# A decoder block on one Trainium2 core: v split in freed constants' space with the output steps overlapped, and two pairs of the embedding gate's second half by seven products

## The chip, the cores and the metric

The kernel runs on one core of one Trainium2 chip. A core has a matrix engine (PE, with its weight loads shown apart as PEld), a vector engine (DVE), a scalar engine (ACT), GpSimd (POOL) and SyncE (SP), which here only issues DMAs. SBUF is the on-chip memory the engines work from, PSUM the eight banks that matmuls accumulate in. The metric is the device time of one execution in microseconds (us); lower is better.

## The reference, cut to what matters

One decoder layer on x of 256 tokens by 2048 columns, all in float32. Two parts matter here. The first is the end of branch A, the gated linear attention, with 4 heads whose values are 512 wide:

```
o = gla_chunked(q, k, v, log_a)
o = o * lax.rsqrt(jnp.mean(o * o, -1, keepdims=True) + RMS_EPS) * gla_norm_g.astype(f32)
o = (o.reshape(B, S, GLA_V) * jax.nn.silu(gr.astype(f32))).astype(x.dtype)
y_gla = o @ w_branch_gla
```

The second is the very end of the layer, the per-layer embedding:

```
x = x + jax.nn.sigmoid(x @ w_ple_gate[i]) * (p[i] @ w_ple_proj[i])
```

Between them lie the second branch, the merge, the output projection, two layer norms and a gated MLP of width 5632. Ahead of the embedding stands the second layer norm, so that its x is the normalised result of the MLP.

## The kernel before, in words

**How a product is made.** Every float32 factor is split into a high part (ACT copies it to the matmul's reduced float32, `copy`, L112) and a low part (DVE subtracts, for weights in `prep`, L220). A product is then three matmuls: high by high, high by low, low by high. Weights come in 284 units of 128 rows by 2048 columns (1 MB). `prep` loads a unit as two halves of 512 KB over SP's queue into `raw` (5 buffers) and splits them into `hi` and `lo` tiles (6 buffers each). `unit(ahead=3)` hands out the next unit and prepares up to three ahead; a preparation starts when a `hi` tile comes free, that is when PE has finished with an older unit. SP works in the order written; the other engines' order is made by a planner, which takes the instruction that is ready by its own estimate of time, earlier program text first.

**Two ways to multiply.** Where weights are the moving operand, a unit is a pair of 128-row blocks by 1024 columns against two token blocks. The classic way (`x_mm`, L333, or `classic` in `s_half`, L792) is 2 x 2 x 2 block products of three matmuls, 24 matmuls of 512 columns. The other way (`strassen` in `s_half`) has seven block products instead of eight, 21 matmuls. It needs sums of activation blocks (`s_sums`, four DVE additions), differences of weight blocks (`differences`, L148, four DVE subtractions of 512 columns), and splits 3584 columns of weights instead of 2048 (`prep_s`, L194). Its products accumulate partly in four more PSUM banks `p1`, `p5`, `p6`, `p7`, which `fold` (L819) adds into an SBUF tile after the last such pair of a half; what the classic pairs gave is added by the evacuation. The projections `gv` and `gr`, the output projection `wo` and the MLP's `dn` are made so; the embedding's gate `pg` is not.

**The output steps of branch A.** After `gv` and `gr`, which fill `vg[h]` (v and the swish gate of head h), come the last 12 merge gates `psm` (n = 20 to 31). Each is 16 pairs of a 512-column and a 256-column matmul. Between their matmuls the generator `o_gen` is pulled one step at a time, twice per gate from n = 21. For each head in turn its steps are: `split` (v and the attention matrix into high and low parts: tiles `vs`, `ath`, `atl`), a pause, `product` (9 matmuls `go`; ACT squares and sums, DVE and POOL make the root, DVE scales and gates, L965), a pause, `turn` (8 PE transposes `gt`, then a split into `oT[h]`). One head is done before the next begins, 5 pulls each. `vs` is a tile of the pool `big`, 15 slots of 8 KB per partition that also hold xT (4 slots), `ofT` (2), the attention matrices (1), the gates `sg` (4), `vg` (4) and `oT` (4). A slot of `xT` is free when the last merge gate has read it. The branch projections `psa` follow and read `oT`.

**Constants' space.** Masks and other constants of the early stages lie in a pool `ec` that stays open until the merge gates are done; the norm's gain `gnb` is one of them.

**The embedding gate.** `pg` is two halves of 1024 columns, each 8 units, by `x_half`. The first half begins inside the second layer norm (`begin2`) and ends with the evacuation of its four banks: ACT's tanh from PSUM (L1460), two DVE steps (L1461, L1463), and a 256 KB store. The store is not issued there but kept in a list; `store_first` issues the four on SP's queue after the second half's first unit. In the second half the last two units are taken bank by bank, so that three banks are evacuated while PE works on the next. The fourth bank is split in two tiles of 256 columns (`fine`) for all eight units, so that its first half can be evacuated while PE makes the second. The last evacuation and its store end the program.

Of the kernel before, what the change touches and what calls it, by code (L numbers as in the profile page):

```python
# [9 lines left out]
F32 = mybir.dt.float32  # L10
# [9 lines left out]
P = 128  # L20
# [41 lines left out]
DN_T = ((3, 6, 9, 12, 15, 18), (5, 9, 12, 15))  # L62
AFF1 = ((0, 2, 3), (0, 2))
# [9 lines left out]
def tile_block(ctx: ExitStack, tc: tile.TileContext, wu, wfv, wpp, xT_in, x_in, pT_in, wlr,  # L73
# [17 lines left out]
    ec = early.enter_context(tc.tile_pool(name="ec", bufs=1))  # L91
    pmm = ctx.enter_context(tc.tile_pool(name="pmm", bufs=6, space=PSUM))
# [28 lines left out]
    for _ in range(8):  # L121
# [7 lines left out]
               for b, order, sset in ((52, WO_ORDER, GV_S), (68, WO_ORDER, GR_S),  # L129
                                      (120, OUT_ORDER, WO_S), (dn0, DN_ORDER, DN_S))  # L130
# [125 lines left out]
    gnb = ec.tile([P, 512], F32, name="gnb")  # L256
# [513 lines left out]
    def s_half(nm, nh, order, sset, cl, st, zof, ev, tail=0, mid={}, end=None, ahead=3,  # L770
               residual=True):
# [19 lines left out]
        def mm(ps, x, w):  # L791
            nc.tensor.matmul(ps, lhsT=x, rhs=w, start=todo[id(ps)] == total[id(ps)],  # L792
                             stop=todo[id(ps)] == 1)
            todo[id(ps)] -= 1
# [48 lines left out]

        if tail:
            end(tail_mm)
            return
# [59 lines left out]

    vg = [s8([P, 2, 2, 512], name=f"vg{h}") for h in range(H)]
# [28 lines left out]
    def o_gen():  # L936
        parts, ogs = {}, {}

        def split(h):
            vs = s8([P, 2, 2, 512], F32R, name=f"vs{h}")  # L940
            copy(vs[:, 0], vg[h][:, 0])
            nc.vector.tensor_tensor(vs[:, 1], vg[h][:, 0], vs[:, 0].bitcast(F32), ALU.subtract)
# [5 lines left out]
        def product(h):  # L948
            vs, ah, al = parts.pop(h)
            for t in range(2):  # L950
                po = mxtile(f"go{h}_{t}")
                ks = ((0, 0),) if t == 0 else ((256, 0), (128, 1))
                mm = [(x[:, o:o + P], vs[:, i, s, :]) for o, s in ks
# [23 lines left out]
        for h in range(H):  # L977
            split(h)
            yield
            yield  # L980
            product(h)
            yield
            yield
            turn(h)
            yield
# [12 lines left out]
    for n in range(PSM1, 32):  # L998
        merge_gate(n, lambda i: pull(1) if i in (3, 11) and n > PSM1 else None)
# [447 lines left out]
    stores = []  # L1447

    def store_first():
        for store in stores:  # L1450
            store()

    for nh in range(2):
        def ev_o(t, c, ps, ab=(0, 512), nh=nh):
            th = t2("tho")
            r = t2("res")
            e = slice(*ab)
            w = slice(c * 512 + ab[0], c * 512 + ab[1])
            o = slice(nh * 1024 + w.start, nh * 1024 + w.stop)
            nc.scalar.activation(th[:, e], ps, AF.Tanh, bias=0.0, scale=0.5)  # L1460
            nc.vector.scalar_tensor_tensor(th[:, e], th[:, e], 1.0, pp[nh][:, t, w],  # L1461
# [114 lines left out]
```

## Time and profile before

| | us |
|---|---|
| median of 3 runs | 1661.32 (1660.44 to 1662.15) |
| the profiled execution: its own time | 1661.22 |
| its span, first to last instruction | 1659.4 |
| PE busy | 1652.1 |
| PEld busy | 1434.6 |
| DVE busy | 1307.9 |
| ACT busy | 899.8 |
| POOL busy | 71.2 |

The span leaves out 1.8 us of the execution's time. Matmuls are pipelined and the profile models their ends, so a busy PE says little by itself: two matmuls that follow without a gap are shown overlapping, and a short wait can hide inside the overlap. What counts for PE is the distance between the starts of its matmuls. Names like `psm` or `go` are the program's tiles, with buffer numbers left out; `L965` is line 965 of the kernel.

### The profile page before, as it was taken

How to read it: one execution, taken by the hardware profiler on the slowest of the kernel's cores; microseconds unless marked ns; L12 is line 12 of the kernel's file. 1: busy time of each engine (PE TensorE's matmuls, PEld its weight loads, DVE VectorE, ACT ScalarE, POOL GpSimd, SP SyncE). 2: the span in 40 equal slices, each digit the busy share in tenths (PEclk: the TensorE clock that was granted, in tenths of full speed). 3: DMA queues.
4: the chain of work that ended last, by engine and by line, in shares of the span. 5: the costliest groups of instructions: out<-in, count | busy, mean ns of one | idle time of the engine just before them, and what ended most of it. 6: DMA issues, size and time to landing. Idle time of an engine off the chain costs nothing.

```text
span 1659.4 us, 24382 instructions
## 1 busy us (share of the span) xinstructions
PE 1652.1 (100%) x8917; PEld 1434.6 (86%) x8917; DVE 1307.9 (79%) x1983; ACT 899.8 (54%) x1314; POOL 71.2 (4%) x210
## 2 busy tenths in 40 slices
PE   9999999999999999999999999999999999999998
PEld 9988888888888888888898888888888888888887
DVE  7666877888889767888987877777777778988774
ACT  6655555555555654455575455555545556556543
POOL 0100000000000000000010101100111000000000
PEclk9999999999999999999999999999999999999999
DMA  8755555546566556878856877778677679898554
GB/s 322 254 165 169 170 175 173 185 158 201 199 205 203 186 187 250 307 241 306 314 172 204 274 269 268 265 243 290 241 263 253 237 268 339 288 363 312 177 187 156
DMA packets 103432, 391.61 MB, mean 236 GB/s; under 512 B 11736, under 2 KB 13024, under 8 KB 96400
## 3 DMA queue, kind: packets, MB, share of 16 engines
q1 hardware_dynamic: 98448, 363.83, 64.3%
q0 software_dynamic: 4864, 26.23, 4.2%
q8 instruction: 70, 1.15, 0.3%
q14 instruction: 50, 0.41, 0.1%
HBM read 362.74 MB, written 27.27 MB: 235 GB/s over the span
## 4 chain that ended last, share of the span: by engine, by line
PE 98%; DVE 1%; ACT 0%; issue 0%; POOL 0%; POOLq 0%; DVEq 0%; ACTq 0%
PE dn L792 10%; PE psu L287 10%; PE psg L287 9%; PE psm L287 7%; PE pg L333 5%; PE psu L289 5%; PE psg L289 5%; PE gv L792 4%; PE gr L792 4%; PE wo L792 4%; PE psm L289 4%; PE dn_p L792 3%; PE psa L287 3%; PE fv L452 3%; PE psfk L287 2%; PE psk L287 2%
## 5 line engine op out<-in xcount | busy, mean ns | idle before, releaser
L220 DVE TENSOR_TENSOR lo<-raw,hi 128x1024 fp32r<-128x1024 f32 x490 | 595.0, 1220 | 192.8 <-ACT hi L112 190.7
L112 ACT ACTIVATE hi<-raw 128x1024 fp32r<-128x1024 f32 x490 | 516.0, 1057 | 380.3 <-issue 143.5
L287 PE MATMUL psu<-x1T,hi 128*128 128x512 f32 x688 | 240.4, 392 | 0.0
L287 PE MATMUL psg<-x1T,hi 128*128 128x512 f32 x672 | 234.8, 392 | 0.0
L289 PE MATMUL psu<-x1T,lo 128*128 128x256 f32 x688 | 192.3, 280 | 0.0
L289 PE MATMUL psg<-x1T,lo 128*128 128x256 f32 x672 | 187.8, 280 | 0.0
L287 PE MATMUL psm<-xT,hi 128*128 128x512 f32 x512 | 181.4, 396 | 0.0
L287 PEld LDWEIGHTS psu<-x1T,hi 128*128 128x128 f32 x688 | 129.2, 188 | 27.6
L287 PEld LDWEIGHTS psg<-x1T,hi 128*128 128x128 f32 x672 | 126.2, 188 | 27.0
L289 PE MATMUL psm<-xT,lo 128*128 128x256 f32 x512 | 143.3, 280 | 0.0
L289 PEld LDWEIGHTS psu<-x1T,lo 128*128 128x128 f32 x688 | 130.6, 190 | 0.0
L289 PEld LDWEIGHTS psg<-x1T,lo 128*128 128x128 f32 x672 | 127.6, 190 | 0.0
L287 PEld LDWEIGHTS psm<-xT,hi 128*128 128x128 f32 x512 | 96.2, 188 | 19.7
L792 PE MATMUL dn<-hi,hC 128*128 128x512 f32 x368 | 102.3, 389 | 0.0
L289 PEld LDWEIGHTS psm<-xT,lo 128*128 128x128 f32 x512 | 97.1, 190 | 0.2
L112 ACT ACTIVATE hi_b<-raw 128x512 fp32r<-128x512 f32 x78 | 65.3, 841 | 53.5 <-DMA raw<-in_wu_dram 19.8
L112 ACT ACTIVATE hi_t<-raw 128x1024 fp32r<-128x1024 f32 x48 | 51.0, 1063 | 75.5 <-DVE raw L148 51.1
L287 PE MATMUL psa<-oT,hi 128*128 128x512 f32 x256 | 89.8, 392 | 0.0
L194 DVE TENSOR_TENSOR lo_b<-raw,hi_b 128x512 fp32r<-128x512 f32 x78 | 73.7, 952 | 15.4 <-ACT hi_b L112 15.3
L792 PEld LDWEIGHTS dn<-hi,hC 128*128 128x128 f32 x368 | 69.0, 188 | 14.4
L289 PE MATMUL psa<-oT,lo 128*128 128x256 f32 x256 | 71.6, 280 | 0.0
L333 PE MATMUL pg<-hi,x2T 128*128 128x512 f32 (+1 forms) x256 | 69.7, 380 | 0.0
(366 smaller groups left out, 3199.5 us busy)
## 6 DMA issues: line engine op xcount, KB each, us to landing
raw<-in_wu_dram SPq DMA_DIRECT2D x553, 512.0 KB, 5.1
td<-in_wu_dram SPq DMA_DIRECT2D x15, 1024.0 KB, 8.5
td<-td POOLq DMA_DIRECT2D x15, 1024.0 KB, 6.5
td<-td SPq DMA_DIRECT2D x15, 1024.0 KB, 8.2
hS<-sd SPq DMA_DIRECT2D x21, 512.0 KB, 8.2
fvraw<-in_wfv_dram SPq DMA_DIRECT2D x13, 524.0 KB, 6.6
sd<-hs POOLq DMA_DIRECT2D x24, 256.0 KB, 5.7
lnb<-in_lng_dram SPq DMA_DIRECT2D x4, 1024.0 KB, 10.3
```

The source lines that it names most:

```text
L112: return nc.scalar.activation(o, i, AF.Copy, bias=0.0, scale=scale)
L194: nc.vector.tensor_tensor(lo, src, hi.bitcast(F32), ALU.subtract)
L220: i = nc.vector.tensor_tensor(lo, raw, hi.bitcast(F32), ALU.subtract)
L287: nc.tensor.matmul(ps, lhsT=hi[i // 8 if hoff == 0 else 0][:, w0 % 1024:w0 % 1024 + P], rhs=a[:, kt % 4, :], start=first and i == 0, stop= ...
L289: nc.tensor.matmul(ps[:, 256:512], lhsT=lo[i // 8 if hoff == 0 else 0][:, w0 % 1024:w0 % 1024 + P], rhs=a[:, kt % 4, 0:256], start=False, ...
L333: nc.tensor.matmul(bs[j][:, 0:m], lhsT=x, rhs=v[:, o:o + m], start=first and i == 0, stop=last and i == 2)
L452: nc.tensor.matmul(fbk[t][c][:, 0:n], lhsT=x, rhs=w[:, o:o + n], start=kt == 0 and i == 0, stop=kt == 15 and i == 2)
L792: nc.tensor.matmul(ps, lhsT=x, rhs=w, start=todo[id(ps)] == total[id(ps)], stop=todo[id(ps)] == 1)
```

## The change

Three parts of the program are changed.

1. **Output steps.** The pool `ec` is cut in two: `gnb` stays, the other constants move to an inner pool that is closed before `gv`. In the freed space `split` now makes v's high part (`vh`, one buffer for both token blocks) and the low part of the first token block (`vl`); the low part of the second takes one of the six small tiles `t2`. No slot of `big` is used, and the subtraction is two of 512 columns instead of one of 1024. `o_gen` runs 19 steps in which heads overlap: head h is split at step 4h, multiplied at 4h + 2, turned at 4h + 5, with `turn` ahead of the other two within a step.
2. **Embedding gate's second half.** It goes through `s_half`, with pairs 2 and 4 by seven products. `g_sums` makes the sums of those pairs after unit 4 of the first half. The result is gathered in an SBUF tile `zg` (by `fold`), to which the evacuation `ev_g` adds each bank before the tanh. The fourth bank is one tile until the last two units; those put their upper 256 columns in a further bank `half`, which is added at the very end.
3. **First half's stores.** They are issued by GpSimd, each right after its evacuation, instead of four on SP's queue in the second half.

The weights are laid out on the host to match. The core of the diff:

```diff
 DN_T = ((3, 6, 9, 12, 15, 18), (5, 9, 12, 15))
+PG_ORDER = (tuple(range(8)), tuple(range(8)))
+PG_S = ((), (2, 4))
 AFF1 = ((0, 2, 3), (0, 2))
...
     ec = early.enter_context(tc.tile_pool(name="ec", bufs=1))
+    gnb = ec.tile([P, 512], F32, name="gnb")
+    first_ = ctx.enter_context(ExitStack())
+    ec = first_.enter_context(tc.tile_pool(name="ec2", bufs=1))
     pmm = ctx.enter_context(tc.tile_pool(name="pmm", bufs=6, space=PSUM))
...
                for b, order, sset in ((52, WO_ORDER, GV_S), (68, WO_ORDER, GR_S),
-                                      (120, OUT_ORDER, WO_S), (dn0, DN_ORDER, DN_S))
+                                      (120, OUT_ORDER, WO_S), (dn0, DN_ORDER, DN_S),
+                                      (NU - 16, PG_ORDER, PG_S))
                for nh in range(2) for i, n in enumerate(order[nh]) if n in sset[nh]}
...
     cmask = ec.tile([P, 256], F32, name="cmask")
-    gnb = ec.tile([P, 512], F32, name="gnb")
     reset = ec.tile([P, 256], F32, name="reset")
...
     def s_half(nm, nh, order, sset, cl, st, zof, ev, tail=0, mid={}, end=None, ahead=3,
-               residual=True):
+               residual=True, fine=False):
...
-        def mm(ps, x, w):
-            nc.tensor.matmul(ps, lhsT=x, rhs=w, start=todo[id(ps)] == total[id(ps)],
+        def mm(ps, x, w, e=slice(0, 512)):
+            nc.tensor.matmul(ps[:, e], lhsT=x, rhs=w, start=todo[id(ps)] == total[id(ps)],
                              stop=todo[id(ps)] == 1)
...
+        if fine:
+            for t, c in ((0, 0), (0, 1), (1, 0)):
+                for i in range(tail):
+                    tail_mm(t, c, i)
+            half = mmtile(f"{nm}{nh}_11b")[:, 0:256]
+            last = [(x, v[:, 512:1024]) for i in range(tail) for j in range(2)
+                    for ah, al in (cl(order[n - tail + i], j, 1),)
+                    for x, v in ((ah, us[i][0][j]), (ah, us[i][1][j]), (al, us[i][0][j]))]
+            for x, v in last:
+                mm(C[1][1], x, v[:, 0:256], slice(0, 256))
+            for k, (x, v) in enumerate(last):
+                nc.tensor.matmul(half, lhsT=x, rhs=v[:, 256:512], start=k == 0,
+                                 stop=k == len(last) - 1)
+            ev(1, 1, C[1][1], half)
+            return
         if tail:
...
+    first_.close()
+    ec = early.enter_context(tc.tile_pool(name="ec3", bufs=1))
     vg = [s8([P, 2, 2, 512], name=f"vg{h}") for h in range(H)]
...
         def split(h):
-            vs = s8([P, 2, 2, 512], F32R, name=f"vs{h}")
-            copy(vs[:, 0], vg[h][:, 0])
-            nc.vector.tensor_tensor(vs[:, 1], vg[h][:, 0], vs[:, 0].bitcast(F32), ALU.subtract)
+            vh = ec.tile([P, 2, 512], F32R, tag="vh", name=f"vh{h}")
+            copy(vh, vg[h][:, 0])
+            vl = [ec.tile([P, 512], F32R, tag="vl", name=f"vl{h}"),
+                  sm.tile([P, 512], F32R, tag="t2", bufs=6, name="vl1")]
+            for t in range(2):
+                nc.vector.tensor_tensor(vl[t], vg[h][:, 0, t], vh[:, t].bitcast(F32),
+                                        ALU.subtract)
+            vs = [(vh[:, t], vl[t]) for t in range(2)]
             ah, al = [sm.tile([P, 384], F32R, tag="t2", bufs=6, name=n) for n in ("ath", "atl")]
...
                 ks = ((0, 0),) if t == 0 else ((256, 0), (128, 1))
-                mm = [(x[:, o:o + P], vs[:, i, s, :]) for o, s in ks
+                mm = [(x[:, o:o + P], vs[s][i]) for o, s in ks
                       for x, i in ((ah, 0), (ah, 1), (al, 0))]
...
-        for h in range(H):
-            split(h)
-            yield
-            yield
-            product(h)
-            yield
-            yield
-            turn(h)
+        for k in range(19):
+            for f, o in ((turn, 5), (product, 2), (split, 0)):
+                h, r = divmod(k - o, 4)
+                if r == 0 and 0 <= h < H:
+                    f(h)
             yield
...
     for n in range(PSM1, 32):
-        merge_gate(n, lambda i: pull(1) if i in (3, 11) and n > PSM1 else None)
+        merge_gate(n, lambda i: pull(1) if i in (3, 11) and 2 * n + i // 8 > 2 * PSM1 + 1 else None)
     while mixers:
...
-    stores = []
-    def store_first():
-        for store in stores:
-            store()
-    for nh in range(2):
-        def ev_o(t, c, ps, ab=(0, 512), nh=nh):
-            th = t2("tho")
-            r = t2("res")
-            e = slice(*ab)
-            w = slice(c * 512 + ab[0], c * 512 + ab[1])
-            o = slice(nh * 1024 + w.start, nh * 1024 + w.stop)
-            nc.scalar.activation(th[:, e], ps, AF.Tanh, bias=0.0, scale=0.5)
-            nc.vector.scalar_tensor_tensor(th[:, e], th[:, e], 1.0, pp[nh][:, t, w],
-                                           ALU.add, ALU.mult)
-            nc.vector.scalar_tensor_tensor(r[:, e], th[:, e], 0.5, z2[nh][:, t, w],
-                                           ALU.mult, ALU.add)
-            store = lambda: nc.sync.dma_start(out[t, :, o], r[:, e])
-            if nh == 0:
-                stores.append(store)
-            else:
-                store()
-        x_half(f"pg{nh}", x2T, 16, ev_o, pulls=2, begin=begin2 if nh == 0 else None,
-               tail=2 if nh == 1 else 0, mid=((mid3, 4), (store_first, 0))[nh],
-               fine=nh == 1)
+    def put(z, nh, t, c, ab=(0, 512)):
+        th = t2("tho")
+        r = t2("res")
+        e = slice(*ab)
+        w = slice(c * 512 + ab[0], c * 512 + ab[1])
+        o = slice(nh * 1024 + w.start, nh * 1024 + w.stop)
+        nc.scalar.activation(th[:, e], z, AF.Tanh, bias=0.0, scale=0.5)
+        nc.vector.scalar_tensor_tensor(th[:, e], th[:, e], 1.0, pp[nh][:, t, w],
+                                       ALU.add, ALU.mult)
+        nc.vector.scalar_tensor_tensor(r[:, e], th[:, e], 0.5, z2[nh][:, t, w],
+                                       ALU.mult, ALU.add)
+        (nc.gpsimd if nh == 0 else nc.sync).dma_start(out[t, :, o], r[:, e])
+    def g_cl(pair, j, t):
+        kt = 2 * pair + j
+        a = x2T[kt // 4][:, kt % 4, :]
+        return a[:, t * P:t * P + P], a[:, 256 + t * P:256 + t * P + P]
+    gS_ = {}
+    def g_sums():
+        for i, pair in enumerate(PG_S[1]):
+            o = s8([P, 4, 256], F32R, name=f"gS{pair}")
+            a = x2T[pair // 2][:, pair % 2 * 2:pair % 2 * 2 + 2, :].bitcast(F32)
+            y = t2("gy").rearrange("p (k t) -> p k t", t=S)
+            nc.vector.tensor_tensor(y, a[:, :, 0:256], a[:, :, 256:512], ALU.add)
+            v = s_sums(y)
+            copy(o[:, :, 0:P], v)
+            nc.vector.tensor_tensor(o[:, :, P:256], v, o[:, :, 0:P].bitcast(F32), ALU.subtract)
+            gS_[pair] = o
+    def g_st(pair, i):
+        if i < 3:
+            return g_cl(pair, (0, 1, 1)[i], (0, 0, 1)[i])
+        return cell(gS_[pair], i - 3)
+    zg = s8([P, 2, 2, 512], name="zg")
+    def ev_g(t, c, ps, half=None):
+        z = zg[:, t, c, :]
+        es = (slice(0, 512),) if half is None else (slice(0, 256), slice(256, 512))
+        for e in es:
+            nc.vector.tensor_tensor(z[:, e], z[:, e], ps[:, e], ALU.add)
+        for e in es:
+            if e.start:
+                nc.vector.tensor_tensor(z[:, e], z[:, e], half, ALU.add)
+            put(z[:, e], 1, t, c, (e.start, e.stop))
+    def mid4():
+        mid3()
+        g_sums()
+    x_half("pg0", x2T, 16, lambda t, c, ps: put(ps, 0, t, c), pulls=2,
+           begin=begin2, mid=(mid4, 4))
+    s_half("pg", 1, PG_ORDER[1], PG_S[1], g_cl, g_st, lambda t, g: zg[:, t, g - 2, :], ev_g,
+           2, {}, residual=False, fine=True)
     assert n_used[0] == NU, (n_used[0], NU)
...
            _sst(i["w_down"][0], DN_ORDER, DN_S),
-           _xst(i["w_ple_gate"][0])], 0)
+           _sst(i["w_ple_gate"][0], PG_ORDER, PG_S)], 0)
     wfv = np.concatenate([c("fv", 1024), c("glr", 16), c("ff", 8)], 1)
```

## Prediction

> **What bounds the kernel now.** I read the page's engine totals first, then the chain that ended last.
>
> ```profile
> span 1659.4 us, 24382 instructions
> PE 1652.1 (100%) x8917; PEld 1434.6 (86%) x8917; DVE 1307.9 (79%) x1983; ACT 899.8 (54%) x1314; POOL 71.2 (4%) x210
> ...
> PE 98%; DVE 1%; ACT 0%; issue 0%; POOL 0%; POOLq 0%; DVEq 0%; ACTq 0%
> ```
>
> The chain is PE for 98% of the span, so a change pays in two ways only: by taking matmuls away, or by closing one of the few places where PE waits; and it costs where PE newly waits, or behind the last matmul. Next come the prices of a matmul, from the chain in order of time (start, length, what).
>
> ```profile
> 421.86 6.12 PE gv L792 x27
> ...
> 1641.28 1.71 PE pg L333 x8
> 1644.06 8.24 PE pg L333 x36
> ```
>
> 27 matmuls of 512 columns take 6.12 us, 0.227 us each, and three of the last four banks (36 matmuls) take 8.24, 0.229 each: PE runs without gaps in both. The row at 1641.28 is one 128-row block of the second gate half: from its start to 1644.06 are 2.78 us, where 12 x 0.227 = 2.72. The difference is the fourth bank, made as 2 x 256 columns.
>
> The Trainium skill, in "TensorE: Matmul & The Clock Gate", section "Wait — 56ns, not 53.3ns?", gives a matmul a fixed cost of about 2.5 ns beside its columns. By that page merging 36 pairs of 256 columns would be worth an estimated 36 x 2.5 ns = 0.09 us instead of the 0.72 worked out below, and my time would be 1659.7. The row shows 60 ns per 3 pairs, 20 ns each, so I go by the row.
>
> Then PE's own timeline around the output steps (the bracket is idle time and who ended it):
>
> ```profile
> 549.12 0.63 PE L956 MATMUL go<-vs,ath 128*128 128x512 f32 x2
> 550.18 0.50 PE L956 MATMUL go<-vs,atl 128*128 128x512 f32 x1 [0.43 <-DVE atl L945]
> ...
> 610.68 0.40 PE L287 MATMUL psm<-xT,hi 128*128 128x512 f32 x1
> 611.51 0.66 PE L974 MATMUL gt<-ident,og 128*128 128x128 f32 x4 [0.43 <-DVE gst L961]
> ...
> 612.36 0.28 PE L289 MATMUL psm<-xT,lo 128*128 128x256 f32 x1
> 613.05 0.66 PE L974 MATMUL gt<-ident,og 128*128 128x128 f32 x4 [0.41 <-DVE og L965]
> ...
> 619.70 0.39 PE L287 MATMUL psa<-oT,hi 128*128 128x512 f32 x1
> 620.39 0.66 PE L974 MATMUL gt<-ident,og 128*128 128x128 f32 x4 [0.30 <-DVE og L965]
> ```
>
> By starts, the last three waits cost 0.83 - 0.23 = 0.60, 0.69 - 0.11 = 0.58 and 0.69 - 0.23 = 0.46 us: 1.64 in all. The first, at head 0's product, costs 1.06 - 0.45 = 0.61. DVE and ACT show why the three stand together.
>
> ```profile
> 560.46 1.23 DVE L942 TENSOR_TENSOR vs<-vg,vs 128x1024 fp32r<-128x1024 f32 x1 [0.45 <-ACT vs L112]
> ...
> 605.88 1.06 ACT L112 ACTIVATE vs<-vg 128x1024 fp32r<-128x1024 f32 x1
> 607.00 1.21 DVE L942 TENSOR_TENSOR vs<-vg,vs 128x1024 fp32r<-128x1024 f32 x1
> ...
> 613.98 1.22 DVE L942 TENSOR_TENSOR vs<-vg,vs 128x1024 fp32r<-128x1024 f32 x1
> ```
>
> Head 1's `vs` is made at 560, head 2's not before 606, although v had been there since `gv` and a head takes five pulls, 8 matmul pairs apart (8 x 0.34 = 2.8 us). At that time the 15 slots of `big` hold xT 4, ofT 2, attention 1, sg 4, vg 2, oT 2: all 15. Head 2 gets a slot when the last merge gate has left the first part of xT, and heads 2 and 3 are squeezed into the end, each PE step right behind its DVE and POOL chain.
>
> **The change part by part. Output steps.** Without `vs` in `big` nothing waits for xT: head 2's product frees a `vg` slot, which `oT[2]` takes. At one pull per 2.8 us head 3's turn, step 17, comes near 600 us, inside the merge gates. Three steps, 8.3 us, now lie between product and turn. The chain between them, below, is 2.1 us from PE's start to `og`'s end for a whole bank (609.10 to 611.45 in the squeezed case, for the first token block), so the three waits, 1.64 us, should go. Against that: head h + 1's product now follows head h's turn after one step instead of three, and needs the two PSUM tiles that the turn used.
>
> ```profile
> 609.10 0.60 ACT L959 ACTIVATE sq<-go 128x512 f32<-128x512 f32 x1 [0.62 <-PE go L956]
> ...
> 610.70 0.75 DVE L965 SCALAR_TENSOR_TENSOR og<-go,gst,vg 128x512 f32<-128x512 f32 x1 [0.73 <-POOL gst L963]
> ...
> 557.45 1.04 PE L974 MATMUL gt<-ident,og 128*128 128x128 f32 x8
> 558.72 1.29 DVE L992 TENSOR_TENSOR oT<-gt,oT 128x512 fp32r<-128x512 f32 x2
> ```
>
> After a turn at 557.45 its tiles are read by 560.01, 2.6 us later; the next product would come 0.9 + 2.8 = 3.7 us after it. 1.1 us of slack covers one DVE split in front (1.23) almost, so I take 0 for this new wait and keep 3 x 0.5 us as its upper bound. Head 0's wait (0.61) is DVE being busy; the two subtractions of 512 that replace one of 1024 cost 2 x 0.69 against 1.23, and I leave that wait as it is, between 0 and 1.2. The part gives -1.6, between -2.3 and +0.5.
>
> **Embedding gate, PE.** Two pairs by 21 matmuls instead of 24 save 6 x 0.227 = 1.36 us. The fourth bank in one piece saves 0.06 x 12 blocks = 0.72; its last two units stay split. Together -2.1.
>
> **Embedding gate, the engines that feed PE.** A seven-product unit costs DVE three splits of 1024 and one of 512 and four differences, 3 x 1.23 + 0.69 + 4 x 0.69 = 7.1 us, against 2.5 classic: +9.3 for two. The sums cost 2 x (0.69 + 4 x 0.28 + 0.69) = 5.0, the fold 4 x 0.68 = 2.7; ACT gets under 5. The cover (window, its length, busy time of PE, PEld, DVE), and the rows of the small steps (mean ns behind the comma):
>
> ```profile
> 454.00:537.00 83.00, 83.00 (x369) 68.71 (x368) 75.65 (x89) 46.74 (x51) 0.00 (x0) 1.00 0.61 200
> ...
> 1588.00:1600.00 12.00, 12.00 (x56) 9.97 (x55) 11.33 (x15) 6.29 (x9) 0.00 (x0) 1.00 0.58 190
> 1600.00:1611.00 11.00, 11.00 (x51) 9.09 (x50) 5.79 (x6) 4.96 (x6) 0.00 (x0) 1.00 0.18 62
> 1611.00:1622.00 11.00, 11.00 (x60) 9.34 (x59) 5.51 (x8) 2.76 (x5) 0.00 (x0) 1.00 0.56 197
> 1622.00:1633.00 11.00, 11.00 (x62) 9.43 (x61) 8.27 (x7) 6.67 (x7) 0.00 (x0) 1.00 0.95 337
> 1633.00:1644.00 11.00, 11.00 (x61) 9.49 (x60) 3.99 (x4) 3.18 (x3) 0.00 (x0) 1.00 0.11 40
> ...
> L749 DVE TENSOR_TENSOR sums<-yp x30: 279/291/293, 646.4 to 1268.9; 128x128 f32<-128x128 f32 x30
> ...
> L148 DVE TENSOR_TENSOR raw<-raw 128x512 f32<-128x512 f32 x22 | 15.2, 691 | 0.7
> ...
> L1362 DVE TENSOR_TENSOR z<-z,dn 128x512 f32<-128x512 f32 x8 | 5.3, 681 | 6.3 <-PE dn L792 6.3
> ```
>
> From 1600 to 1644 DVE is busy 23.6 of 44 us. With 17.0 more it is busy 40.6: 92%. The window from 454 is `gr`, three seven-product units per half, DVE at 91%, and PE has no wait in it. So I take 0 for PE, but the cover is thin: by slots, the first such unit's last splits are done about 2.6 us before PE needs them. If a wait does come, it is what DVE is then behind.
>
> **Embedding gate, the end.** This part costs. Here is the end before:
>
> ```profile
> 1652.32 0.60 ACT L1460 ACTIVATE tho<-pg 128x512 f32<-128x512 f32 x1 [2.12 <-PE pg L333]
> 1652.95 0.69 DVE L1461 SCALAR_TENSOR_TENSOR tho<-tho,ppk 128x512 f32<-128x512 f32 x1 [1.30 <-ACT tho L1460]
> ...
> 1654.87 0.28 PE L333 MATMUL pg_11b<-hi,x2T 128*128 128x256 f32 x1
> 1655.19 0.38 ACT L1460 ACTIVATE tho<-pg_11b 128x256 f32<-128x256 f32 x1 [1.05 <-DVE res L1463]
> 1655.60 0.43 DVE L1461 SCALAR_TENSOR_TENSOR tho<-tho,ppk 128x256 f32<-128x256 f32 x1 [0.45 <-ACT tho L1460]
> 1656.06 0.43 DVE L1463 SCALAR_TENSOR_TENSOR res<-tho,z 128x256 f32<-128x256 f32 x1
> ```
>
> Let 0 be the end of the last matmul (1655.15). Before, the third bank is ready at -2.8 and the last DVE step ends at +1.3. After, each bank first needs a DVE addition, of 0.68 (that of `dn`, above) or, for 256 columns, about 0.43 like the steps of that size, then tanh, then the two steps. From -2.8 on DVE has: third bank's addition to -2.1; a gap of 0.6 for its tanh; its two steps to -0.05; three additions for the fourth bank, which overlap a little, to about +1.0; four steps every 0.46, to +2.8. So the tail is 1.5 us longer, if the planner puts the last addition ahead of the first steps; if DVE takes it behind them and the last tanh stands exposed, 2.2 longer. I take +1.5, since the planner fills DVE where something is ready.
>
> **First half's stores.** SP now:
>
> ```profile
> 1611.43 5.71 SPq L1465 DMA_DIRECT2D out_dram<-res  x4
> 1617.24 13.91 SPq L216 DMA_DIRECT2D raw<-in_wu_dram  x10
> ...
> 1621.24 1.06 ACT L112 ACTIVATE hi<-raw 128x1024 fp32r<-128x1024 f32 x1 [8.24 <-DMA raw<-in_wu_dram]
> ```
>
> The four stores wait on SP for DVE, the ten loads behind them start at 1617, and ACT waits 8.24 us. PE does not wait, so moving them gives 0 by itself; but without it the larger preparations would start 6 us late. GpSimd has nothing else to do there, and the stores have some 40 us to land: 0.
>
> **Sum.** -1.6 - 2.1 + 1.5 = -2.2 against the profiled execution's own 1661.2 (span 1659.4 and 1.8 around it), which stands at the median, 1661.3: **1659.1**.
>
> **Rivals.** *The waits give more:* head 0's wait goes too (-0.6) and the tail grows by 0.7 instead of 1.5: 1661.3 - 2.2 - 0.6 - 0.8 = 1657.7, and down to 1657 if the plain rate of 0.227 also holds where the second half begins. For it: the atl split it waits for is queued behind weight splits that the planner may order anew. *The change does not do what it says in the output steps:* the new PSUM wait (3 x 0.5) eats the 1.6, and the tail costs 2.2: 1661.3 - 0.1 - 2.1 + 2.2 = 1661.3. For it: product and turn now stand one step apart. Against it: 1.1 us of slack. *DVE becomes the bound of the second gate half (slower):* the first seven-product unit can use only the slots that classic units free, the second those of the first, so DVE stands idle for about two units' PE time, 2 x 4.8 = 9.6, in a half where it has about 31 us to do (two units 14.2, less one split and a half done early; three more classic units and the last 7.3; fold 2.7; the first half's evacuation 5.5) before the last two units at 31.3: they would come some 8 us late, at 1661.3 - 2.2 + 8 = 1667. It decides once DVE enters the second half more than 2.6 us behind. For it: window 1588 to 1600 just ahead is DVE's densest in this stage; against it: `gr` at 91% without a wait.
>
> The skill's "Perfetto Trace Analysis", section "Identifying the Most-Contended Engine", holds matmul busy time a bad measure and would judge PE's headroom by weight loads. By that page the 86% would leave PE room and removed matmuls might save nothing, at an estimated 1661.2; the distance between starts, 0.227 us without a gap, speaks against it, and I give it no chance of its own.
>
> **How the numbers follow.** A measurement of this kernel can tell about 0.2% (3.3 us) from no change. Forecast 0.54, its own range 1657.4 to 1660.6, of which about a quarter lies under 1658.0; more 0.18; eaten up 0.15; DVE-bound 0.13. Faster: 0.18 x 0.9 + 0.54 x 0.26 = 0.30; slower 0.13; the rest, 0.57, within. The range from 1656.8 to 1662.2 leaves out the DVE case and some of the gains.
>
> **What would show it.** Right: third and fourth `vh` made by about 590, transposes `gt` over by about 603 and no PE wait near 610 to 620; 42 matmuls at 0.227 us in the two units and no split bank until the end; from the last matmul's start to the last DVE step 3.1 us instead of 1.6; loads on SP running on at 1611. Wrong: a PE wait on `go` for `gt`'s readers, or on `lo_t` or `hi_t` in the gate's second half; a tail of 4 us or more.

## The result, and the profile after

| | us |
|---|---|
| before, median of 13 runs | 1661.32 (1660.44 to 1662.85) |
| after, median of 13 runs | 1657.59 (1657.37 to 1658.05) |
| ratio | 0.9978, 95% interval 0.9971 to 0.9985 |
| the profiled execution after: its own time, its span | 1657.66, 1655.9 |

The change made the kernel 3.7 us faster, 0.22%: little more than the 0.2% that the prediction took as the least that can be told from no change, but the interval lies clear of 1. The forecast was 1659.1.

The page of the kernel after, the totals and the chain by engine:

```profile
PE 1648.5 (100%) x8875; PEld 1432.1 (86%) x8875; DVE 1326.3 (80%) x2021; ACT 904.7 (55%) x1321; POOL 73.0 (4%) x214
...
PE 98%; DVE 1%; DMA 0%; ACT 0%; issue 0%; POOL 0%; SPq 0%; DVEq 0%; POOLq 0%
```

42 matmuls fewer, DVE 18 us busier, and PE still carries 98% of the chain. So the question is again where PE's distances between starts shrank, and what stands behind its last matmul. I cut both profiled executions at the same four places: the last matmul of `gr`, the first of `wo`, the first of the gate `pg`, and the gate's last.

| stretch, us | before | after | difference |
|---|---|---|---|
| start to last `gr` | 536.41 | 536.40 | 0.0 |
| to first `wo`: the output steps | 214.61 | 211.98 | -2.63 |
| to first `pg`: the rest | 813.10 | 813.15 | +0.05 |
| first to last start in `pg` | 90.75 | 88.36 | -2.39 |
| to the end of the last DVE step | 1.62 | 2.82 | +1.20 |
| to the end of the span: the last store | 2.93 | 3.15 | +0.22 |

These add up to the span's 3.55 us. Now each place. First, all that PE waited for in the kernel after, by the view of waits:

```profile
PE warm_ps L127 <- DVE warm L124: 1.2, 1, 1.2
PE fv L457 <- ACT fvhi L117: 0.3, 1, 0.3
```

Both belong to the start of the program. The waits on `og`, `gst` and `atl`, which the prediction quotes, are gone, and none has come in the gate. PE's timeline after, where head 0 is multiplied and where its turn and head 1's product follow:

```profile
549.11 0.39 PE L983 MATMUL go<-vh,ath 128*128 128x512 f32 x1
549.34 0.40 PE L983 MATMUL go<-vl,ath 128*128 128x512 f32 x1
549.58 0.49 PE L983 MATMUL go<-vh,atl 128*128 128x512 f32 x1
549.91 0.39 PE L983 MATMUL go<-vh,ath 128*128 128x512 f32 x1
...
559.64 1.04 PE L1001 MATMUL gt<-ident,og 128*128 128x128 f32 x8
...
563.30 0.40 PE L983 MATMUL go<-vh,ath 128*128 128x512 f32 x1
```

The third product matmul starts 0.24 us behind the second, where some 0.6 us more were lost before. The turn is one piece of eight transposes, and the next product starts 3.66 us after it and without a gap: the new wait for the turn's PSUM tiles has not come. ACT's timeline after shows when v's high part is made:

```profile
414.60 1.06 ACT L117 ACTIVATE vh<-vg 128x1024 fp32r<-128x1024 f32 x1 [1.10 <-DVE vg L935]
...
566.23 1.05 ACT L117 ACTIVATE vh<-vg 128x1024 fp32r<-128x1024 f32 x1
580.32 1.05 ACT L117 ACTIVATE vh<-vg 128x1024 fp32r<-128x1024 f32 x1
```

The third and fourth are made at 566 and 580, not behind xT at 606 and later; head 0's is made at 414.6, as soon as `gv` has given v. That is where head 0's wait most likely went. DVE's timeline at that place, first before, then after:

```profile
538.63 2.47 DVE L928 TENSOR_TENSOR vg<-vg,gr 128x512 f32<-128x512 f32 x4
...
549.58 0.54 DVE L945 TENSOR_TENSOR atl<-at,ath 128x384 fp32r<-128x384 f32 x1
```

```profile
537.41 2.47 DVE L950 TENSOR_TENSOR vg<-vg,gr 128x512 f32<-128x512 f32 x4
...
548.36 0.68 DVE L967 TENSOR_TENSOR vl<-vg,vh 128x512 fp32r<-128x512 f32 x1
548.97 0.55 DVE L972 TENSOR_TENSOR atl<-at,ath 128x384 fp32r<-128x384 f32 x1
```

Only one subtraction of head 0 is left in this crowded stretch, and DVE reaches `gr`'s evacuation 1.2 us and `atl` 0.6 us sooner.

In the gate, the chain of the kernel after has PE without gaps (start, length, what):

```profile
1607.86 10.88 PE pg L797 x48
...
1633.02 8.86 PE pg L797 x39
```

That is 0.227 us a matmul in both rows. DVE's share by windows, in the columns of the prediction's windows. The gate stands 2.6 us earlier now, so these windows are moved by 3 us to cover the same stage:

```profile
1586.00:1597.00 11.00, 11.00 (x50) 9.09 (x49) 11.00 (x23) 6.26 (x9) 0.00 (x0) 1.00 0.36 112
1597.00:1608.00 11.00, 11.00 (x50) 9.09 (x50) 9.17 (x12) 4.55 (x7) 0.00 (x0) 1.00 0.77 253
1608.00:1619.00 11.00, 11.00 (x50) 9.13 (x49) 10.58 (x14) 5.82 (x8) 2.20 (x4) 1.00 0.54 173
1619.00:1630.00 11.00, 11.00 (x50) 9.10 (x49) 9.14 (x10) 6.52 (x8) 0.00 (x0) 1.00 0.67 197
1630.00:1641.00 11.00, 11.00 (x50) 9.12 (x49) 8.25 (x9) 4.60 (x6) 0.00 (x0) 1.00 0.26 91
```

From 1597 to 1641 DVE is busy 37.1 of 44 us, 84%, and all 11 us of the window ahead. The end after, all engines but SP's queue and the weight loads:

```profile
1649.67 0.69 DVE L1480 SCALAR_TENSOR_TENSOR res<-tho,z 128x512 f32<-128x512 f32 x1
...
1649.89 0.28 PE L860 MATMUL pg_11b<-hi,x2T 128*128 128x256 f32 x1
1650.27 0.41 DVE L1513 TENSOR_TENSOR zg<-zg,pg 128x256 f32<-128x256 f32 x1
...
1650.60 0.42 DVE L1478 SCALAR_TENSOR_TENSOR tho<-tho,ppk 128x256 f32<-128x256 f32 x1
1650.94 0.41 DVE L1516 TENSOR_TENSOR zg<-zg,pg_11b 128x256 f32<-128x256 f32 x1
1651.27 0.42 DVE L1480 SCALAR_TENSOR_TENSOR res<-tho,z 128x256 f32<-128x256 f32 x1
1651.39 0.42 ACT L1477 ACTIVATE tho<-zg 128x256 f32<-128x256 f32 x1 [1.18 <-DVE zg L1516]
1651.83 0.43 DVE L1478 SCALAR_TENSOR_TENSOR tho<-tho,ppk 128x256 f32<-128x256 f32 x1
1652.29 0.42 DVE L1480 SCALAR_TENSOR_TENSOR res<-tho,z 128x256 f32<-128x256 f32 x1
```

The last matmul is over at 1650.17. The addition that waits for it (L1516) starts at 1650.94, because DVE is still at the third bank's last step and the fourth bank's earlier ones. From there the chain is addition, tanh, two steps.

### The profile page after: what moved, and what is told of

It reads as the page before. It is cut to its first block, busy times and chain, and to the rows that moved or that the text cites. A ratio compares the mean times of both kernels' runs of the same rounds, so it can differ in the third digit from the quotient of the medians.

```text
span 1655.9 us, 24358 instructions
## 1 busy us (share of the span) xinstructions
PE 1648.5 (100%) x8875; PEld 1432.1 (86%) x8875; DVE 1326.3 (80%) x2021; ACT 904.7 (55%) x1321; POOL 73.0 (4%) x214
## 4 chain that ended last, share of the span: by engine, by line
PE 98%; DVE 1%; DMA 0%; ACT 0%; issue 0%; POOL 0%; SPq 0%; DVEq 0%; POOLq 0%
PE dn L797 10%; PE psu L292 10%; PE psg L292 9%; PE psm L292 7%; PE psu L294 5%; PE psg L294 5%; PE gv L797 4%; PE gr L797 4%; PE wo L797 4%; PE psm L294 4%; PE psa L292 4%; PE dn_p L797 3%; PE pg L338 3%; PE fv L457 2%; PE psa L294 2%; PE psk L292 2%
## 5 line engine op out<-in xcount | busy, mean ns | idle before, releaser
L117 ACT ACTIVATE hi_t<-raw 128x1024 fp32r<-128x1024 f32 x52 | 55.2, 1062 | 80.8 <-DVE raw L154 57.9
L117 ACT ACTIVATE hi_b<-raw 128x512 fp32r<-128x512 f32 x82 | 68.7, 841 | 54.9 <-DMA raw<-in_wu_dram 12.9
L200 DVE TENSOR_TENSOR lo_b<-raw,hi_b 128x512 fp32r<-128x512 f32 x82 | 77.8, 953 | 15.8 <-ACT hi_b L117 15.7
L200 DVE TENSOR_TENSOR lo_t<-raw,hi_t 128x1024 fp32r<-128x1024 f32 x52 | 63.5, 1222 | 10.4 <-ACT hi_t L117 8.8
```

The lines of the kernel that those rows point to most:

```text
L117: return nc.scalar.activation(o, i, AF.Copy, bias=0.0, scale=scale)
L200: nc.vector.tensor_tensor(lo, src, hi.bitcast(F32), ALU.subtract)
```

## The experiments

Eleven kernels, eleven runs each but for ten of the last, in four sessions with the kernel before in each (its medians: 1660.86 for the first four rows, 1660.99 for the next four, then 1660.91, 1660.91 and 1660.70). "Output" is the stretch from the last `gr` to the first `wo`, "PE" that from the first to the last start in `pg`, "tail" and "store" the two behind it, each from the profiled execution. The start of the program differs by up to 1.3 us between these executions, so stretches are compared, not spans; medians of different sessions are compared by their distance from their own before.

| kernel | median | ratio to before, 95% | output | PE | tail | store |
|---|---|---|---|---|---|---|
| output steps only | 1658.93 | 0.9989 (0.9980 to 0.9998) | 211.88 | 90.75 | 1.62 | 2.92 |
| gate only | 1660.34 | 0.9997 (0.9989 to 1.0006) | 214.38 | 88.38 | 2.82 | 3.14 |
| space, old order | 1657.66 | 0.9981 (0.9972 to 0.9989) | 211.88 | 88.35 | 2.82 | 3.15 |
| order, old space | 1660.12 | 0.9997 (0.9988 to 1.0006) | 214.62 | 88.37 | 2.82 | 3.16 |
| three pairs | 1657.64 | 0.9982 (0.9973 to 0.9990) | 211.93 | 87.70 | 4.14 | 3.15 |
| one pair | 1658.46 | 0.9984 (0.9975 to 0.9992) | 211.88 | 89.06 | 2.82 | 3.15 |
| stores on SP | 1658.23 | 0.9987 (0.9978 to 0.9996) | 211.88 | 90.10 | 2.82 | 2.93 |
| one addition on GpSimd | 1657.37 | 0.9978 (0.9969 to 0.9987) | 211.88 | 88.38 | 2.47 | 3.14 |
| four additions on GpSimd | 1657.59 | 0.9980 (0.9971 to 0.9988) | 211.88 | 88.40 | 2.57 | 3.39 |
| that, three pairs | 1661.22 | 1.0003 (0.9994 to 1.0012) | 211.88 | 91.42 | 2.78 | 3.39 |
| three additions on GpSimd | 1657.12 | 0.9977 (0.9968 to 0.9986) | 211.88 | 88.35 | 2.41 | 3.16 |

**The two parts alone.** The kernel before with the output steps of the change, and the kernel before with the gate and the stores of the change; the edits are those of the diff above.

> The kernel before with the output steps' part alone (freed constants' space for the split of v, overlapping heads); the embedding gate and its stores as before. Theory: from the start of the branch projections on, PE's starts came 2.6 us earlier in the changed kernel, and the rest of the gain came in the gate. So 1661.3 - 2.6 = 1658.7 us, with no wait of PE at go and gt. Rival: the earlier steps only pay because the gate's end also changed, that is, an earlier middle is given back at the end: 1661.3.

> The kernel before with the gate's second half by two seven-product pairs and the first half's stores on GpSimd; the output steps as before. Theory: PE saves 2.4 us in the second half (6 matmuls, the fourth bank in one piece, and the waits for banks at its start), the DVE tail behind the last matmul gives back 1.2 to 1.5: 1660.2 us, between 1659.9 and 1660.6. Rival, the tail eats all that PE saves: 1661.3.

The output steps alone shorten their stretch by 2.73 us and leave the gate as it was; the gate alone shortens PE's part by 2.37, lengthens tail and store by 1.20 and 0.21, and leaves the output stretch within 0.23 of the old. The medians, -1.9 and -0.5 us, are each smaller than these stretches say (-2.7 and -1.0), and add up to 2.4 of the 3.7 us; each interval is about 1.5 us to either side, so the medians can't settle it. In both profiled executions the start was late, by 0.8 and 1.3 us; whether it was in the others is not shown. By the stretches the parts do not act on each other: those of the two kernels together are those of the kernel after.

**Space or order.** Two kernels split the output steps. In the first, `o_gen` runs head by head as before, but in the freed space:

```diff
-        for k in range(19):
-            for f, o in ((turn, 5), (product, 2), (split, 0)):
-                h, r = divmod(k - o, 4)
-                if r == 0 and 0 <= h < H:
-                    f(h)
+        for h in range(H):
+            split(h)
+            yield
+            yield
+            product(h)
+            yield
+            yield
+            turn(h)
             yield
```

> The changed kernel with the old order of the output steps (one head after the other, 5 pulls each), v still split in the freed constants' space. Theory (slots): the heads were late because vs waited for a slot of big; with no slot needed the old order is enough: 1657.6 to 1657.9, the third vh made by about 585, the last gt by about 607, no PE wait at gt. Rival (order): product and turn two pulls apart and the last head at the very end keep the three waits of 1.64 us: 1659.2. Head 0's wait at its product (0.6 us) is gone in both if it went because vh of head 0 is made early (at 414 us), and is back if it went by the order.

In the second, the overlapped order stays and v goes to `big` again:

```diff
-            vh = ec.tile([P, 2, 512], F32R, tag="vh", name=f"vh{h}")
-            copy(vh, vg[h][:, 0])
...
+            vb = s8([P, 2, 2, 512], F32R, name=f"vs{h}")
+            copy(vb[:, 0], vg[h][:, 0])
+            nc.vector.tensor_tensor(vb[:, 1], vg[h][:, 0], vb[:, 0].bitcast(F32), ALU.subtract)
+            vs = [(vb[:, 0, t], vb[:, 1, t]) for t in range(2)]
```

> The changed kernel with the new overlapping order, but v split in a tile of big as before. Theory (slots): the third head's vs waits until the last merge gate leaves xT, at about 605, whatever the order; the three waits of 1.64 us and, since vs of head 0 is again made in the crowded stretch around 516, the wait of 0.6 come back: 1659.2 to 1659.9. Rival (order): overlapping alone removes them: 1657.6.

The space does it all, 211.88 us as in the other runs, and the order nothing: 214.62 against 214.61 before. The waits of PE in the kernel with the order alone are those of before:

```profile
PE gt L997 <- DVE og L988: 0.7, 2, 0.5
...
PE gt L997 <- DVE gst L984: 0.4, 1, 0.4
PE go L979 <- DVE atl L968: 0.3, 1, 0.3
```

and the third and fourth heads' `vs` on its ACT timeline show why:

```profile
571.85 1.05 ACT L117 ACTIVATE vs<-vg 128x1024 fp32r<-128x1024 f32 x1
...
608.58 1.05 ACT L117 ACTIVATE vs<-vg 128x1024 fp32r<-128x1024 f32 x1
```

The expectation had the third head's late too. The overlapped order frees `vg` slots sooner, so only the fourth head's comes about when xT is left (before, the third head's came at 605.88); but that one is enough to squeeze its product and turn into the end, and head 0's `vs` comes late as before, at 517. So the prediction's reading, that the space and not the sequence of steps set the waits, is shown. The space comes with two smaller subtractions in place of one, and the runs do not try these two apart.

**How many pairs.** The first edit takes three pairs, the second one:

```diff
-PG_S = ((), (2, 4))
+PG_S = ((), (1, 3, 5))
```

```diff
-PG_S = ((), (2, 4))
+PG_S = ((), (2,))
```

> The changed kernel with three pairs (1, 3, 5) of the gate's second half by seven products instead of two. Theory of cover (DVE is off the path): one more pair saves 3 matmuls of 0.227 = 0.7 us, 1656.9. Rival (DVE is at its limit): it is busy 37 of 44 us ahead of the last units in the changed kernel, and a third pair adds 4.6 for splits and differences and 2.5 for sums, 44 of 44; PE then waits for the splits, and the time is 1657.6 or more, up to 1660.

> The changed kernel with one pair (2) of the gate's second half by seven products instead of two. If PE's matmuls alone set the time of this stage: 3 more matmuls of 0.227, 1658.3. If the two pairs' load on DVE costs PE something that no wait shows: less than that, 1657.6 or under.

A pair is worth 0.70 us of PE from one to two and 0.66 from two to three; the prediction's 3 x 0.227 is 0.68. With one and two pairs the tail is the same, so two pairs are wholly paid for. With three, PE does not wait either, although the theory of a DVE at its limit had expected it to. But the gain is lost all the same: the tail is 4.14 instead of 2.82 us, and the median is 3.4 us below its own before, not more than the 3.7 of the kernel after. DVE's windows in the kernel with three pairs:

```profile
1597.00:1608.00 11.00, 11.00 (x50) 9.11 (x49) 10.93 (x15) 4.99 (x7) 0.00 (x0) 1.00 0.60 191
...
1630.00:1641.00 11.00, 11.00 (x50) 9.13 (x49) 10.58 (x12) 6.51 (x7) 0.00 (x0) 1.00 0.33 119
```

With the two windows between (10.96 and 9.56) DVE is busy 42.0 of 44 us, 96%. What it puts off is what PE does not wait for: the folds (four from 1640 on) and the banks' evacuation behind them. Its backlog shows only behind the last matmul. So DVE's limit, the slower rival, exists in this stage, one pair further on and in another place than it was looked for.

**The stores.** The first half's stores go back to SP's queue after the second half's first unit:

```diff
-        (nc.gpsimd if nh == 0 else nc.sync).dma_start(out[t, :, o], r[:, e])
+        store = lambda: nc.sync.dma_start(out[t, :, o], r[:, e])
+        if nh == 0:
+            stores.append(store)
+        else:
+            store()
...
-           2, {}, residual=False, fine=True)
+           2, {0: store_first}, residual=False, fine=True)
```

> The changed kernel with the first half's four stores back on SP's queue, kept in a list and issued after the second half's first unit. Theory of the prediction: the loads behind the waiting stores start late, and with the larger preparations PE then waits, 1 us or more: 1658.6 and above. Rival: in the changed kernel the loads that would stand behind the stores start at 1617.5 us anyway, since they wait for a raw buffer, and the stores would be gone by then: 1657.6, no wait of PE.

SP's queue in this kernel, then what PE waited for in the gate:

```profile
1609.16 7.56 SPq L1488 DMA_DIRECT2D out_dram<-res  x4
...
1617.78 0.96 SPq L188 DMA_DIRECT2D raw<-in_wu_dram  x2
```

```profile
PE pg_p L797 <- DVE lo_t L200: 0.8, 1, 0.8
```

The loads of the second seven-product unit (L188) stand at 1617.78 behind the stores. In the kernel after they are ahead, and the stores, the last of them in the second fence, pass by on GpSimd:

```profile
1604.81 8.76 SPq L188 DMA_DIRECT2D raw<-in_wu_dram  x2
1617.51 4.00 SPq L222 DMA_DIRECT2D raw<-in_wu_dram  x3
```

```profile
1616.65 0.54 POOL L1482 DMA_DIRECT2D out_dram<-res  x1 [0.53 <-DVE res L1480]
```

With the stores on SP, ACT makes that unit's two `hi_t` at 1627.6 and 1631.3 instead of 1624.3 and 1625.8, PE loses 1.74 us in this execution, and the end of the store is 0.22 shorter. The median is 2.8 us below its own before, against 3.7 for the kernel after, and the intervals overlap; its runs spread from 1657.96 to 1661.63, so this wait may not be the same in every execution. What the prediction said of the stores, nothing by themselves but needed by the larger preparations, holds in the profiled execution; the medians are too close to show it.

**What the tail is made of.** GpSimd takes over last additions of banks, from halves of `pp` and sums made ahead. In the first kernel that is the third bank's alone; in the second, all but that of the last half bank, with the sums made on GpSimd too; the third is the second with three pairs whose operand sums GpSimd makes; in the fourth both halves of the last bank stay with DVE. The edit of the second:

```diff
+        if nh == 1 and (t, c, ab[0]) != (1, 1, 256):
+            nc.vector.tensor_tensor(th[:, e], th[:, e], pp[nh][:, t, w], ALU.mult)
+            nc.gpsimd.tensor_tensor(r[:, e], th[:, e], z2[nh][:, t, w], ALU.add)
+        else:
...
+    def ahead_():
+        for t in range(2):
+            e = slice(0, 1024 if t == 0 else 768)
+            a, b = pp[1][:, t, e], z2[1][:, t, e]
+            copy(a, a, 0.5)
+            nc.gpsimd.tensor_tensor(b, b, a, ALU.add)
...
-           2, {}, residual=False, fine=True)
+           2, {1: ahead_}, residual=False, fine=True)
```

The first and the fourth have, in place of its condition, `nh == 1 and (t, c) == (1, 0)` and `nh == 1 and (t, c) != (1, 1)`. The first has one sum of 512 columns, made by DVE after unit 5, and the fourth sums 1024 and 512 columns. The third has this:

```diff
-PG_S = ((), (2, 4))
+PG_S = ((), (1, 3, 5))
...
-            nc.vector.tensor_tensor(y, a[:, :, 0:256], a[:, :, 256:512], ALU.add)
-            v = s_sums(y)
+            nc.gpsimd.tensor_tensor(y, a[:, :, 0:256], a[:, :, 256:512], ALU.add)
+            v = s_sums(y, nc.gpsimd)
```

> The changed kernel with the third bank's last addition moved from DVE to GpSimd: half of p's projection and its sum with z are made ahead, while DVE is idle, so that the bank needs tanh, one DVE product and one GpSimd addition. Theory (the tail is bound by DVE's amount of work): from the last matmul's start to the last DVE step 2.2 instead of 2.8 us, 1657.0. Rival (the tail is the chain of the last half bank): unchanged, 1657.6; if GpSimd's addition lands after all else, later.

> Two pairs as in the changed kernel; the last addition of every bank of the gate's second half except the last half bank is made by GpSimd, from halves and sums made ahead (ACT halves, GpSimd adds). If the tail behind the last matmul is DVE's backlog of work: DVE loses six passes of about 0.7 us, the tail goes from 2.83 us to about 2.1 us (the bare chain of the last half bank), matmuls unchanged, and the time is about 1656.9 us. If GpSimd's passes (1.27 us each in the run with one of them) hold up DVE or the stores instead, the tail stays at 2.8 us or more and the time is 1657.4 us or above.

> The run before with three pairs, whose operand sums are made by GpSimd instead of DVE. If three pairs gained nothing only because DVE had no time left: the gate's matmuls take 0.6 us less as in the run with three pairs, the tail stays at about 2.1 us, and the time is about 1656.3 us. If DVE is still behind with the folding of a third pair's products, the tail is 3 us or more and the time 1657 us or above.

> Two pairs; GpSimd makes the last addition of the three whole banks of the gate's second half, and both halves of the last bank stay with DVE. In the run with GpSimd also on the first half of the last bank, DVE's last step took 0.83 us instead of 0.42 beside a GpSimd addition, and the tail was 2.57 us. If the two engines hold each other up, DVE's last step is back at 0.42 us here; DVE makes one 0.42 us step more ahead of it, which puts the last chain back by about 0.2 us: tail about 2.35 us, time about 1657.3 us. If the longer last step had another cause (its operands, its place), it stays at 0.8 us and the tail is 2.8 us, time 1657.7 us.

One last addition less on DVE shortens the tail by 0.35 us. Four fewer should have brought it to the bare chain of 2.1, but gave 2.57. The end of the kernel with four, DVE and POOL:

```profile
1650.30 0.42 DVE L1520 TENSOR_TENSOR zg<-zg,pg_11b 128x256 f32<-128x256 f32 x1
...
1651.28 0.99 POOL L1480 TENSOR_TENSOR res<-tho,z 128x256 f32<-128x256 f32 x1 [0.36 <-DVE tho L1479]
1651.72 0.83 DVE L1484 SCALAR_TENSOR_TENSOR res<-tho,z 128x256 f32<-128x256 f32 x1
```

The backlog is gone, as supposed: the last addition starts at 1650.30, right behind the last matmul. But the last step takes 0.83 us instead of 0.42, beside a GpSimd addition. With GpSimd kept off the last bank that step is 0.42 again, and the tail 2.41, where 2.35 was expected:

```profile
1652.30 0.42 DVE L1484 SCALAR_TENSOR_TENSOR res<-tho,z 128x256 f32<-128x256 f32 x1
```

Without the 0.41 us of holding up, the bare chain would be an estimated 2.57 - 0.41 = 2.16 us. So, by this estimate, of the 1.20 us that the tail grew, 0.54 are the longer chain (2.16 against 1.62: an addition ahead of the tanh) and 0.66 are DVE's backlog, of which the runs took off 0.41 at most. Three pairs on top failed: PE now waits, chiefly for `lo` and `lo_t`, and loses 3.7 us against three pairs with DVE's own sums. From 1597 to 1641 DVE is busy 42.6 of 44 us there, and the last section shows what GpSimd passes do to it in the kernel with four additions. But DVE had also stood idle for 2.5 us just ahead, from 1592.4 to 1594.9, by the profile waiting for ACT; in the kernel with three pairs and DVE's own sums it is busy throughout. Which of these the 3.7 us come from was not tried apart. The kernels with three additions and with one on GpSimd have the lowest medians, 1657.12 and 1657.37, against 1657.59 of the kernel after. But against their own before both gain 3.6 us and the kernel after 3.7, and the intervals overlap, so none is shown to beat it.

## Why the prediction was right, and where its sizes were off

The sign, the place of the gain and its causes came out as worked out; the sum was -2.2 us and the profile has -3.55. By steps:

- *Output steps, the three waits at the end: -1.64.* Right in cause and place (slots of `big`, shown by the kernels with the space alone and the order alone). The step that failed is the next one: "I leave that wait as it is", for head 0's 0.61 us. It is gone in the kernel after, 0.59 by starts, in the kernel with the space alone too, and back with the old space: the kernel after makes head 0's high part and half of the low part 100 us earlier, out of the stretch in which DVE was late. That is 1.64 + 0.59 = 2.23 of the 2.63. The rest is spread over small delays that stood in no term. In the kernel before, for one, the matmul behind head 0's wait starts at 550.18, in a row that the prediction shows, and the next is this:

```profile
550.52 0.62 PE L956 MATMUL go<-vs,ath 128*128 128x512 f32 x2
```

  That is 0.34 us instead of 0.23. And the four transposes behind each of the last three waits take 0.66 us, where four out of a row without a wait would take 0.60 (3 x 0.11 from start to start and 0.27 for the last). The delay at head 0's product is still there in the kernel after, where no wait is shown (549.58 to 549.91, 0.33 us). Where these delays come from was not tried.
- *The new PSUM wait: 0.* Right. The 2.1 us given for the chain between product and turn are 2.35 by its own rows (609.10 to 611.45), and 609.10 is ACT's start, not PE's; with three steps between them this changed nothing.
- *Gate, PE: -2.1.* Measured -2.39. The pairs are worth what was said, by the runs with one and three pairs. One bank in one piece was put at 0.72 from 12 blocks; by the kernel with one pair it is 90.75 - 89.06 - 0.68 = 1.01. Some 0.2 of the difference is at the half's first matmuls, where the old kernel's fourth bank lost more than in the steady part:

```profile
1611.86 0.28 PE L333 MATMUL pg_11b<-hi,x2T 128*128 128x256 f32 x1
1612.07 0.39 PE L333 MATMUL pg<-hi,x2T 128*128 128x256 f32 x1
1612.29 0.51 PE L333 MATMUL pg<-lo,x2T 128*128 128x512 f32 x2
1612.64 0.28 PE L333 MATMUL pg_11b<-lo,x2T 128*128 128x256 f32 x1
1612.76 0.52 PE L333 MATMUL pg<-hi,x2T 128*128 128x512 f32 x2
```

  There the first two matmuls of 256 columns take 0.21 and 0.22 us to the next start, later ones 0.12. What holds them was not tried. The Trainium skill, "TensorE: Matmul & The Clock Gate", section "Wait — 56ns, not 53.3ns?", puts a matmul's fixed cost at about 2.5 ns, which for 36 merged pairs would be an estimated 0.09 us; the runs do not agree, they show 1.01, or about 0.8 without the half's first matmuls. Matmuls taken away did save their time, 0.70 and 0.66 us for three, so the prediction's estimate of nothing for them, from weight loads at 86%, did not come out.
- *Gate, the engines that feed PE: 0 for PE.* Right, with more room than the 92% said: DVE was busy 84% in that stage. "If a wait does come, it is what DVE is then behind" is wrong in one respect: with three pairs DVE was busy 96% of the stage, no wait came, and the price appeared in the tail.
- *The end: +1.5.* Measured +1.20, below both of the ends given. The planner's order was neither of the two: the last addition (1650.94) stands behind one step of the half bank ahead of it and in front of the other, beside which its tanh runs. By the runs with GpSimd about half of it is DVE's backlog, the other half the longer chain.
- *The stores: 0.* PE's part is right. But the end of the span came 0.22 us later behind the last step: 3.14 us or more in every kernel with the first half's stores on GpSimd, 2.92 and 2.93 in every one with them on SP. That cost stood in no term.
- *What would show it.* No wait near 610 to 620, transposes over by 602.7, no split bank until the end: as written; from the last matmul's start to the last DVE step 2.82 us, where 3.1 was said. Loads on SP did not run on at 1611: two stood from 1604.81 to 1613.6 with no store ahead of them, and the next came at 1617.51. That they stood for `raw` buffers is inferred, not tried; PE did not wait for them.

Of the rivals, "the waits give more" was half right and its time, 1657.7, is the measured one: head 0's wait did go, and the plain rate did hold at the start of the second half; the tail it had at +0.7 was +1.20. That its sum hits the time is luck in part: it has the output steps 0.4 and the gate 0.3 us too small, the tail 0.5 and the store 0.2 too cheap, and these cancel. That the output steps gain nothing fell with the first run. That DVE becomes the bound did not happen with two pairs; its mechanism, idle slots between the two units, made no wait with three either. Its sum does not come out as written: the pieces named for the 31 us add up to about 28, and 9.6 + 28 against 31.3 is some 6 us late, not 8, at 1665.

## What to carry to other kernels

When a few late waits stand together, look up which slot each of their first inputs got and from whom: here moving one tile out of a shared pool gave all of 2.7 us, and reordering the same steps gave nothing. Early work has its price at the place it is taken from: an instruction that can move a hundred microseconds ahead also empties the crowded stretch it used to stand in. An engine that feeds the bound one may be nearly full and still cost no wait, because it puts off what nobody waits for yet; then read its backlog behind the last instruction of the bound engine before adding more to it.

## What the runs showed of the hardware

**DVE and GpSimd hold each other up.** A GpSimd addition of 128x512 takes 1.27 to 1.3 us at the end of the gate, where DVE takes 0.69. In the kernel with four additions on GpSimd, the two made ahead (1024 and 768 columns; about 4.5 us by that rate) run while DVE is busy 21.3 of 22 us (1586 to 1608). POOL's row, then DVE's:

```profile
1592.28 15.73 POOL L1528 TENSOR_TENSOR z<-z,ppk 128x1024 f32<-128x1024 f32 x2 [33.42 <-DVE z L1151]
```

```profile
1603.64 2.65 DVE L226 TENSOR_TENSOR lo<-raw,hi 128x1024 fp32r<-128x1024 f32 x1 [0.68 <-ACT hi L117]
1606.22 2.33 DVE L200 TENSOR_TENSOR lo_b<-raw,hi_b 128x512 fp32r<-128x512 f32 x1
```

The pair takes 15.7 us (spans on POOL are rough), and two DVE passes that take 1.22 and 0.69 us elsewhere take 2.65 and 2.33; the other DVE passes in that time keep their length. In the kernel with three pairs on GpSimd the same two additions take 2.73 and 3.31 us, so the 15.7 is no fixed price. The Trainium skill, "GPSIMD Engine Reference", section "8. Key points", says that GpSimd shares its SBUF interfaces with VectorE and contends with DVE instructions that have two SBUF inputs; the rows agree, for all of these have two, and so does the last step of 0.83 us above.

**A store's issuer shows at the program's end.** 2.92 us from the last DVE step to the span's end with the first half's stores on SP, 3.14 to 3.16 with them on GpSimd, 3.39 in the two kernels with four additions there. The kernel with the stores on SP differs from the kernel after only in the issuer and the place of those four stores, so the 0.22 go with them (one trace each); why was not tried.
